# A one-core decoder layer: a third token tile that overlaps the second, state updates taken four sequences at a time, FFN rows fetched at another place, and a new order of the first transfers

## The chip, the cores and the metric

The kernel runs on one core of one Trainium2 chip. The metric is the device time in microseconds (us), the median of several runs; lower is better. Engines are named as the profile names them: PE is TensorE (PEld its weight loads), DVE is VectorE, ACT is ScalarE, POOL is GpSimd, SP is SyncE, which here only starts transfers. All numbers are float32 (`F32`) or the faster matmul form of it (`F32R`).

## The reference, cut to what matters

One step of one decoder layer over 256 prompt tokens (one sequence) and 64 sample tokens (8 sequences of 8 tokens), 320 tokens in all, model width 2048:

```python
u = x @ w_in                                   # 2048 -> 6680: q, k, v, o, two gates, z, xBC, dt
h_m, C, n, m = mlstm_mixer(q, k, v, o, ...)    # 4 heads, 256x256 matrix state per sequence and head
h_s, S, sconv = ssd_mixer(z, xbc, dt, ...)     # 16 heads, 64x128 state per sequence and head
x = layer_norm(ALPHA * x + concat(h_m, h_s) @ w_out)
up = x @ w_up                                  # 2048 -> 11008, then a causal convolution of 3 taps
x = layer_norm(ALPHA * x + (silu(g) * val) @ w_down)

# mLSTM, one sequence (chunk):                 # SSD, one sequence (chunk):
num = (q k' * w_intra) @ v + w_inter * (q @ C) # y = (C B' * decay * dt) @ x + exp(b) * (C @ S)
C_new = decay * C + sum(w_end * k v')          # S_new = exp(b_end) * S + sum(w_end * B x')
```

Every sample sequence brings its own states C and S in and takes new ones out: 8 x 4 matrices of 256x256 and 8 x 16 of 64x128.

## The kernel before, in words

**Main work.** Activations lie transposed, features on partitions and the 320 tokens along the free dimension. Each weight matrix is read in 512 KB pieces (`raw`, four buffers, SP queue, line 61) and split into a rounded part `hi` and a remainder `lo` (ACT line 74, DVE line 75, five buffers each). For every 128x128 weight block three F32R matmuls run: hi times XH, hi times XL, lo times XH (all PE work passes through line 232, or 238 for transposes). There are 9456 such main matmuls: 2496 for `w_in`, 768 for `w_out`, and 6192 for the FFN. A quad is one split, four weight blocks or 12 main matmuls.

**Background work.** Everything else (convolutions, gates, the two mixers, norms) is written as Python generators. After every quad `tasks.pump` lets those run whose due time has come; a due time is the sum of rough matmul costs so far (`tasks.clk`) plus what the generator yielded. So the instruction order of every engine is fixed when the program is written, and PE executes one stream in which short bursts of background matmuls stand between quads. An engine that has to wait holds up all that stands behind it in its own stream.

**Tiles of the 320 tokens.** Tokens 0 to 127 and 128 to 255 are full tiles. The third tile is tokens 256 to 319: 64 rows (`tok(i)` gives 128, 128, 64). It is met in the input transposes (line 412), in the score and decay blocks, in the outputs of both mixers, and in norms.

**The parts the change touches.** `x_transpose` (line 403) turns 16 feature blocks of the input, per block two 128x128 prompt transposes and one of 64 sample rows, in calls of four blocks. `ssd_sample` (line 782): per sequence b, transpose its state, multiply it by its decay on POOL (line 816), add the outer products in `update(b, g)`: four matmuls with 32-row operands in rows 32*(b%4) of the array, to one PSUM bank. `ssd_heads` (line 849) builds per pair of heads the outputs; the sample part is the 64x64 block plus two matmuls with the 0/1 matrix `sel`, which pick 8 of every 32 rows of the state's contribution `yi`. `ml_chunks` (line 1131) does the mLSTM states: two tiles of two sequences per turn, three tiles loaded ahead; four sequences of a turn each get their own two 32-row matmuls. `ml_out` (line 1206) adds, per head, scores times v for the three tiles; the third again fetches `yi` through `sel`. `ffn_consts` (line 1339) fetches convolution rows and weights for the FFN in 512-byte pieces on the POOL queue, waits in due time, and transposes them on PE (line 1347).

**Queues.** Weights, states and big outputs go through SP in order; a transfer there waits for a semaphore of an earlier one or for the engine that frees its buffer. POOL issues small transfers between its arithmetic.

Of the kernel before, what the change touches and what calls it, by code (L numbers as in the profile page):

```python
# [13 lines left out]
NT = 320  # L14
# [7 lines left out]
class Stream:  # L22
# [21 lines left out]
    def load(self, upto=None, own=()):  # L44

        own = list(own)
        while self.nr < len(self.raws) and (own or self.live < self.RB):
# [12 lines left out]
            for c in range(0, m, step):  # L60
                (self.nc.sync if self.nr > 1 else self.nc.scalar).dma_start(t[:, :, c:c + step], src[:, :, c:c + step])
# [109 lines left out]
def _hybrid_step(ctx, tc, I, O):  # L171
# [77 lines left out]
    def tok(i):  # L249
        return 128 if i < 2 else 64  # L250
# [3 lines left out]
    sel = cp.tile([128, 2, 64], F32, name="sel")  # L254
# [58 lines left out]
    def diag3(dg, cols_of):  # L313
        for i in range(3):
            n = tok(i)
            V.tensor_scalar(dg[0:n, i, 0:n], ident[0:n, 0:n], cols_of(i)[0:n], None, ALU.mult)
        return dg

    def colbc(dg):

        ps = bank()
        for i in range(3):
            n = tok(i)
            mm(ps[:, 128 * i:128 * i + n], ones[0:n, :], dg[0:n, i, 0:n], True, True)
        return ps
# [75 lines left out]

    def x_transpose(c, kks=range(4)):
# [4 lines left out]
        for kk in kks:  # L407
# [27 lines left out]
    xs_in = mt("T10", [64, D])  # L435
    for c in range(4):
        x_load(c)
        s = slice(512 * c, 512 * c + 512)
        dma(xs_in[:, s], I["x_sample"].rearrange("b t f -> (b t) f")[:, s])
        if c == 0:  # L440
            src = I["x_prompt"][0, :, 256:512].rearrange("(i p) f -> p i f", p=128)
            dma(box["x", 0][:, :, 256:512], src)
            own = [mt("T4", [128, 1024]) for _ in range(4)]
        st.load(2 * c + 2, (own[0:2], own[2:4], (), ())[c])
# [16 lines left out]

    def load_small():
# [14 lines left out]
        hr = mt("T10", [24, 1536])  # L477
        gdma(hr, I["state_ssm_conv"][0].rearrange("b r c -> (b r) c"))
        gdma(c_tm, I["c_tm"])
        gdma(dsk, I["ssm_D"].broadcast_to([128, 16]))  # L480
        gdma(m01, I["c_m01"])
        gdma(sel, I["c_sel"])
# [5 lines left out]
        for i in range(12):  # L488
            transpose(ps[:, 24 * i:24 * i + 24], hr[:, 128 * i:128 * i + 128])
        A.activation(histx, ps[:, 0:288].rearrange("p (a b) -> p a b", b=24), AF.Copy)  # L490
# [20 lines left out]
    def gate_task(pg):  # L511
        gf, gi = mt("T2", [128, 384]), mt("T2", [4, NT])
        V.memset(gf[:, NT:384], 0.0)
        V.tensor_copy(gf[:, 0:NT], pg[:, 0:NT])
# [5 lines left out]
        for i in range(3):  # L520
            mm(pt[:, 24 * i:24 * i + 24], gf[:, 128 * i:128 * i + 128], fold[:, 0:24], True, True)
        pf = bank()
        mm(pf[0:4, 0:NT], fold[:, 0:4], gf[:, 0:NT], True, True)
# [36 lines left out]
        transpose(pd[0:48, 0:64], dt3[0:64, 2, :])  # L560
# [4 lines left out]
        V.tensor_copy(dtf[32:48], pd[32:48, 0:64])  # L565
# [47 lines left out]
        for i in range(3):  # L613
            transpose(p1[:, 128 * i:128 * i + 128], T1[:, 128 * i:128 * i + 128])
        A.activation(TT1, p1[:, 0:384].rearrange("p (a b) -> p a b", b=128), AF.Copy)
        p2 = bank()
# [59 lines left out]
    def ssd_cb():  # L676
# [4 lines left out]
        for g in range(2):  # L681
# [3 lines left out]
            mm(ps[0:64, 384:448], B[:, g, 256:NT], C[:, g, 256:NT], True, True)  # L685
            t = mt("T2", [128, 448])
            G.memset(t[64:128, 384:448], 0.0)
            V.tensor_tensor(t[:, 0:384], ps[:, 0:384], m01[:, 0:384], ALU.mult)
            V.tensor_tensor(t[0:64, 384:448], ps[0:64, 384:448], m01[0:64, 384:448], ALU.mult)
# [76 lines left out]
    def ssd_xdt():  # L766
# [3 lines left out]
        for i in range(3):  # L770
            n = tok(i)
            for hh in range(2):
                ps = bank()
                for j in range(4):
                    transpose(ps[0:n, 128 * j:128 * j + 128], XS[:, 4 * hh + j, 128 * i:128 * i + n])
                V.tensor_tensor(by(xdt[0:n, i, 512 * hh:512 * hh + 512], 64), by(ps[0:n, :], 64),
                                bcl(dt3[0:n, i, 32 + 8 * hh:40 + 8 * hh], 64), ALU.mult)
                yield 500
        box["xdt"] = xdt
        flags.add("xdt")  # L780

    def ssd_sample():
# [19 lines left out]
        yield from wait("bc")  # L802
        load(0)
        load(1)
        yield from wait("x4")
        yi = {}
        for b in range(8):
            t = tiles[b]
            sts[b] = mt("T4", [128, 8, 128])
            for g in range(2):  # L810
# [6 lines left out]
                yield 1000  # L817
            if b:
                update(b - 1, 0)
                yield 500  # L820
                update(b - 1, 1)
                yield 1000
            if b > 1:
                dma(s_dst[b - 2].rearrange("(j q) n -> q j n", q=128), tiles.pop(b - 2))
            if b < 6:
                load(b + 2)
            if b % 4 == 3:
                x = b // 4
                for g in range(2):
                    ps = bank()  # L830
                    for c in range(4):
                        w = sts[4 * x + c][:, 4 * g:4 * g + 4, :].rearrange("p j n -> p (j n)")
                        mm(ps[32 * c:32 * c + 32, :], box["cz"][:, g, 4 * x + c, :], w, True, True)
                    y = mt("T2", [128, 512])
                    V.tensor_tensor(by(y, 64), by(ps, 64), bcl(eb[:, x, 8 * g:8 * g + 8], 64), ALU.mult)
                    yi[g, x] = y
                    yield 0
                sts.clear()
        update(7, 0)
        yield 0  # L840
        update(7, 1)
        box["yi"] = yi
        flags.add("yi")
        yield
        for b in (6, 7):
            dma(s_dst[b].rearrange("(j q) n -> q j n", q=128), tiles.pop(b))

    def ssd_heads():
# [41 lines left out]
        for j in range(8):  # L890
# [47 lines left out]
    def ssd_norm():  # L938
        var = sm([128, 3, 2])
        G.memset(var, 1.0)  # L940
        for g in range(2):
# [10 lines left out]
            for i in range(3):  # L952
                mm(ps[0:tok(i), 2 * i:2 * i + 2], sq[:, 128 * i:128 * i + tok(i)], ones[:, 0:2], True, True)
            pv = ps[:, 0:6].rearrange("p (a b) -> p a b", b=2)
# [771 lines left out]
```

## Time and profile before

| | |
|---|---|
| runs, median (lowest to highest) | 1579.27 us (1578.6 to 1581.3) |
| the profiled execution's own time | 1580.12 us |
| its span, first to last instruction | 1578.3 us |
| PE / PEld / DVE / ACT / POOL busy, share of the span | 98% / 95% / 62% / 49% / 18% |
| granted TensorE clock, mean | 0.992 |
| moved by transfers | 253.97 MB, 161 GB/s over the span |

A row of the timeline gives start and length in us, engine, line, what was computed from what, partitions x elements and a count; in brackets the idle time ahead of it and what ended it. Because matmuls are pipelined, the time one costs PE is the distance from its start to the next start, not its own length. A transpose or an F32R matmul is one record, a full float32 matmul is two. A timeline row can gather forms that differ under the first one's name (a run of 64-row and 128-row transposes has one row). Rows of stretches give, per engine, busy time and records, then the granted clock, the busy share of the transfer engines, and GB/s.

### The profile page before, as it was taken

Reading aid. Unit: us, or ns where it says so; the run is one execution under the profiler, and the core shown is the slowest. Engines: PE = TensorE matmul, PEld = TensorE weight load, DVE = VectorE, ACT = ScalarE, POOL = GpSimd, SP = SyncE. Lnnn points to the kernel's source line nnn. Section 1 sums busy time; section 2 is a strip of 40 time slices with the busy share of each in tenths; the row PEclk is TensorE's granted clock in tenths of the full one; section 3 lists DMA queues with packets and bytes.
Section 4 is the critical chain, followed back from the end, with each engine's and each line's share of the span. In section 5 each row is a group of like instructions: output and inputs, shape, how many; then the busy total and the mean of one; then the engine's idle time right before and its main releaser. Section 6 shows DMA issues by size and latency. Waiting matters only on the chain.

```text
span 1578.3 us, 27987 instructions
## 1 busy us (share of the span) xinstructions
PE 1553.8 (98%) x10547; PEld 1502.5 (95%) x10547; DVE 976.6 (62%) x1957; ACT 773.1 (49%) x1532; POOL 290.3 (18%) x601
## 2 busy tenths in 40 slices
PE   9999999999999997999999999999999999999997
PEld 7999999998889997999999999999999999999996
DVE  5775445656677585687777545565644465556765
ACT  3665433435445453476666435555533455555332
POOL 4213220024311073133321000000000000001301
PEclk9999999999999998999999999999999999999998
DMA  9456665577665566445554455455444545455642
GB/s 260 147 161 160 187 187 172 143 193 208 195 221 183 169 183 138 134 147 149 149 151 135 157 158 146 148 156 152 136 152 144 167 145 151 143 154 168 170 140 79
DMA packets 267080, 253.97 MB, mean 161 GB/s; under 512 B 18804, under 2 KB 261263, under 8 KB 266816
## 3 DMA queue, kind: packets, MB, share of 16 engines
q1 hardware_dynamic: 260432, 246.76, 53.2%
q0 software_dynamic: 4928, 4.37, 1.3%
q8 instruction: 82, 1.34, 0.3%
q10 hardware_dynamic: 1584, 1.05, 0.3%
q14 instruction: 54, 0.44, 0.1%
HBM read 231.63 MB, written 20.43 MB: 160 GB/s over the span
## 4 chain that ended last, share of the span: by engine, by line
PE 86%; issue 7%; DMA 2%; POOL 1%; DVE 1%; ACT 1%; POOLq 0%; SPq 0%; DVEq 0%; ACTq 0%
PE bk L232 84%; PE bk L238 2%; DMA rows<-ffn_conv_w 1%; POOL T L425 1%; DMA raw<-w_out 1%; DVE lo L75 1%; DMA T<-ln_g 0%; DMA gbias<-ssm_dt_bias 0%; DMA xT<-T 0%; POOL big L1654 0%; ACT hi L74 0%; DVE big L1393 0%; DVE big L1389 0%; ACT L657 0%; ACT T L644 0%
## 5 line engine op out<-in xcount | busy, mean ns | idle before, releaser
L75 DVE TENSOR_TENSOR lo<-raw,hi 128x512 fp32r<-128x512 f32 (+2 forms) x800 | 556.4, 706 | 391.7 <-ACT hi L74 389.3
L74 ACT ACTIVATE hi<-raw 128x512 fp32r<-128x512 f32 (+2 forms) x800 | 486.3, 616 | 455.9 <-PE bk L232 427.3
L232 PE MATMUL bk<-big,hi 128*128 128x320 f32 (+1 forms) x2752 | 609.3, 310 | 0.0
L232 PEld LDWEIGHTS bk<-big,hi 128*128 128x128 f32 x2752 | 462.2, 188 | 0.1
L232 PE MATMUL bk<-big,lo 128*128 128x320 f32 (+1 forms) x1376 | 426.5, 310 | 0.0
L232 PE MATMUL bk<-XH,hi 128*128 128x320 f32 x832 | 270.2, 325 | 0.1
L232 PEld LDWEIGHTS bk<-big,lo 128*128 128x128 f32 x1376 | 259.3, 188 | 0.0
L232 PE MATMUL bk<-XH,lo 128*128 128x320 f32 x832 | 258.2, 310 | 0.1
L232 PE MATMUL bk<-XL,hi 128*128 128x320 f32 x832 | 258.0, 310 | 0.0
L232 PE MATMUL bk<-HH,hi 128*128 128x320 f32 x688 | 214.2, 311 | 0.0
L232 PE MATMUL bk<-HH,lo 128*128 128x320 f32 x688 | 212.6, 309 | 0.0
L232 PE MATMUL bk<-HL,hi 128*128 128x320 f32 x688 | 212.5, 309 | 0.0
L232 PEld LDWEIGHTS bk<-XH,hi 128*128 128x128 f32 x832 | 157.2, 189 | 14.7 <-issue 5.5
L232 PEld LDWEIGHTS bk<-XL,hi 128*128 128x128 f32 x832 | 157.4, 189 | 0.4
L232 PEld LDWEIGHTS bk<-XH,lo 128*128 128x128 f32 x832 | 157.2, 189 | 0.6 <-DVE lo L75 0.6
L1492 DVE SCALAR_TENSOR_TENSOR c<-c,fcol,c 128x336 f32<-128x336 f32 x172 | 98.0, 570 | 58.6 <-ACT c L1490 55.6
L232 PEld LDWEIGHTS bk<-HL,hi 128*128 128x128 f32 x688 | 129.2, 188 | 0.0
L232 PEld LDWEIGHTS bk<-HH,hi 128*128 128x128 f32 x688 | 129.2, 188 | 0.0
L232 PEld LDWEIGHTS bk<-HH,lo 128*128 128x128 f32 x688 | 129.1, 188 | 0.0
L193 POOL TENSOR_SCALAR fst<-c 128x18 f32<-128x18 f32 x86 | 22.2, 265 | 567.4 <-ACT c L1485 567.4
L232 PE MATMUL bk<-MH,hi 128*128 128x320 f32 x256 | 80.9, 316 | 0.0
L232 PE MATMUL bk<-MH,lo 128*128 128x320 f32 x256 | 80.1, 313 | 0.7 <-DVE lo L75 0.7
(338 smaller groups left out, 1505.8 us busy)
## 6 DMA issues: line engine op xcount, KB each, us to landing
raw<-ffn_w_up SPq DMA_DIRECT2D x172, 512.0 KB, 3.8
raw<-w_in SPq DMA_DIRECT2D x100, 512.0 KB, 4.1
raw<-ffn_w_down SPq DMA_DIRECT2D x71, 512.0 KB, 3.6
raw<-w_out SPq DMA_DIRECT2D x32, 512.0 KB, 3.9
T<-state_mlstm_C SPq DMA_DIRECT2D x32, 256.0 KB, 5.8
s_C<-T SPq DMA_DIRECT2D x32, 256.0 KB, 4.9
T<-state_ssm SPq DMA_DIRECT2D x8, 512.0 KB, 6.5
s_ssm<-T SPq DMA_DIRECT2D x8, 512.0 KB, 5.3
```

What stands on the lines that cost most here:

```text
L74: nc.scalar.activation(h, src, AF.Copy)
L75: nc.vector.tensor_tensor(l, src, h.bitcast(F32), ALU.subtract)
L193: G.tensor_scalar(out, in_, 1.0, 0.0, ALU.mult, ALU.add)
L232: nc.tensor.matmul(out, lhsT=lhsT, rhs=rhs, start=start, stop=stop)
L238: nc.tensor.transpose(out, in_, ident[b:b + p, b:b + p])
L425: G.tensor_tensor(t, f32(XH(k, 2)), f32(XL(k, 2)), ALU.add)
L1492: V.scalar_tensor_tensor(c[:, 0:336], xp[:, j:j + 336], fcol[:, j, i:i + 1], c[:, 0:336], ALU.mult, ALU.add)
```

## The change

- **Third token tile.** It becomes tokens 192 to 319, 128 rows of which the last 64 (partitions 64 to 127) are the sample tokens. `tok` goes, `TS` gives the three slices. The first 64 rows are duplicates of tokens 192 to 255; in the two places where a sum runs over them they carry something else (next point).
- **State contributions.** In both mixers `yi` is no longer added through `sel`. Four small POOL transfers per tile (`gather`) copy 8 of every 32 rows into the free partitions 0 to 63 of the third tile of `xdt` or `VT`, and the matching 64x64 block of the weights is the identity. One matmul then does both.
- **State updates of four sequences.** `ssd_sample` decays four states, then issues 16 update matmuls per half with the sequence as the inner loop, into four banks; `ml_chunks` issues the eight of a turn likewise, half outside, sequence inside. Four chunk tiles are loaded ahead, and stored and reloaded two at a time.
- **Input.** Sample rows are loaded as 128 partitions (feature halves above each other), so that a transpose serves blocks k and k+8. The first weight pieces move from the ACT queue to SP, the identity and the first sample rows from SP to ACT; nine warm-up matmuls instead of seven.
- **FFN rows.** `ffn_consts` starts its transfers after 12000 instead of 25000 of due time and waits 40000 instead of 20000 before it transposes.

The diff, cut to its core (norms, scores, the final transposes and LN2 use `TS` in the same way):

```diff
-                (self.nc.sync if self.nr > 1 else self.nc.scalar).dma_start(t[:, :, c:c + step], src[:, :, c:c + step])
+                self.nc.sync.dma_start(t[:, :, c:c + step], src[:, :, c:c + step])
-    def tok(i):
-        return 128 if i < 2 else 64
+    TS = (slice(0, 128), slice(128, 256), slice(192, NT))
...
-    for _ in range(7):
+    for _ in range(9):
         mm(warm[:, 0:128], ones, ones, True, True)
...
-            dma(ident, I["c_ident"])
+            nc.scalar.dma_start(ident, I["c_ident"])
...
-            transpose(ps[:, 256:NT], xs_in[:, 128 * k:128 * k + 128])
-            A.activation(XH(k), ps[:, 0:NT], AF.Copy)
-            V.tensor_tensor(XL(k), ps[:, 0:NT], f32(XH(k)), ALU.subtract)
+            parts = [(k, 0, 256)]
+            if k < 8:
+                transpose(ps[:, 256:384], xs_in[:, 128 * k:128 * k + 128])
+                parts = [(k, 0, NT), (k + 8, NT, 384)]
...
+    x_load(0)
+    xs_load(nc.scalar, 0, 256)
+    own = [mt("T4", [128, 1024]) for _ in range(4)]
+    st.load(1, own[0:1])
+    dma(box["x", 0][:, :, 256:512], I["x_prompt"][0, :, 256:512].rearrange("(i p) f -> p i f", p=128))
+    xs_load(nc.sync, 256, 512)
+    st.load(2, own[1:2])
...
+    def gather(out, y):
+        for c in range(4):
+            gdma(out[8 * c:8 * c + 8], y[32 * c:32 * c + 8])
...
-        def update(b, g):
-            v = tiles[b][:, 4 * g:4 * g + 4, :]
-            ps = bank()
-            r = slice(32 * (b % 4), 32 * (b % 4) + 32)
-            for j in range(4):
-                mm(ps[:, 128 * j:128 * j + 128], box["X4"][b // 4][r, 4 * g + j, :], box["B4"][r, b // 4, g, :],
-                   True, True)
-            V.tensor_tensor(v, v, ps.rearrange("p (j n) -> p j n", n=128), ALU.add)
+        def update(x, g):
+            pss = [bank() for _ in range(4)]
+            for j in range(4):
+                for c in range(4):
+                    r = slice(32 * c, 32 * c + 32)
+                    mm(pss[c][:, 128 * j:128 * j + 128], box["X4"][x][r, 4 * g + j, :], box["B4"][r, x, g, :],
+                       True, True)
+            tasks.clk -= 12 * 108
+            for c in range(4):
+                v = tiles[4 * x + c][:, 4 * g:4 * g + 4, :]
+                V.tensor_tensor(v, v, pss[c].rearrange("p (j n) -> p j n", n=128), ALU.add)
+                if g:
+                    dma(s_dst[4 * x + c].rearrange("(j q) n -> q j n", q=128), tiles.pop(4 * x + c))
...
+                gather(box["xdt"][32 * x:32 * x + 32, 2, 512 * g:512 * g + 512], y)
...
-            for x in range(2):
-                mm(ps[:, 256:NT], box["yi"][g, x][:, 128 * (j % 4):128 * (j % 4) + 128], sel[:, x, :], x == 0, False)
             for e, (p, f) in enumerate(pe):
-                mm(ps[p, 256:NT], xdt[0:64, 2, f], mw[e][0:64, 384:448], False, True)
+                mm(ps[p, 256:NT], xdt[:, 2, f], mw[e][:, 384:448], True, True)
             for i in range(2):
-                mm(po, xw[:, i, :], btok[:, i, g, :], i == 0, i == 1)
+                for e, (p, f) in enumerate(pe):
+                    mm(po[p, :], xw[:, i, p], btok[:, i, g, :], i == 0, i == 1)
...
-        for n in range(3):
+        for n in range(4):
             load(n)
...
-                box["yi", h, x] = yi
+                gather(box["VT"][32 * x:32 * x + 32, 2, h, 0:257], yi[:, 0:257])
                 yield 500
+                pss = [bank() for _ in range(4)]
+                for e in range(2):
+                    for b in range(4):
+                        r = slice(32 * b, 32 * b + 32)
+                        mm(pss[b][:, 256 * e:256 * e + 256], kv[r, 0, x, 128 * e:128 * e + 128], kv[r, 1, x, :], True, True)
...
-        mm(ps[0:64, 0:257], P[0:64, 384:448], VT[0:64, 2, h, 0:257], True, False)
-        for x in range(2):
-            mm(ps[0:64, 0:257], sel[:, x, :], box.pop(("yi", h, x))[:, 0:257], False, x == 1)
-        A.activation(num[0:64, 2, 0:257], ps[0:64, 0:257], AF.Copy)
+        mm(ps[:, 0:258], P[:, 384:512], VT[:, 2, h, :], True, True)
+        A.activation(num[:, 2, :], ps[:, 0:258], AF.Copy)
...
     def ffn_consts():
-        yield 25000
+        yield 12000
...
-        yield 20000
+        yield 40000
```

In the program's order the change shows at two places on which the prediction rests. The first is PE, one pair of SSD heads (`ssd_heads`). Names before the arrow are the bank written, after it the moving and then the stationary operand's tile; the numbers are the program's buffer numbers. Before:

```order
L232 MATMUL bk_2964<-T_240_2829,T_156_1738 64x256
L232 MATMUL bk_2964<-T_241_2834,T_156_1738 64x256
L232 MATMUL bk_2964<-T_240_2829,T_156_1738 64x128
L232 MATMUL bk_2964<-T_241_2834,T_156_1738 64x128
L232 MATMUL bk_2964<-sel,T_202_2288 128x64
L232 MATMUL bk_2964<-sel,T_233_2733 128x64
L232 MATMUL bk_2964<-T_240_2829,T_156_1738 64x64
L232 MATMUL bk_2964<-T_241_2834,T_156_1738 64x64
L232 MATMUL bk_2964<-T_149_1720,T_242_2839 128x128 x2
L232 MATMUL bk_2862<-XH_368,hi_2881 128x320
```

And now, for such a pair:

```order
L232 MATMUL bk_2951<-T_243_2799,T_156_1730 64x256
L232 MATMUL bk_2951<-T_244_2804,T_156_1730 64x256
L232 MATMUL bk_2951<-T_243_2799,T_156_1730 64x128
L232 MATMUL bk_2951<-T_244_2804,T_156_1730 64x128
L232 MATMUL bk_2951<-T_243_2799,T_156_1730 64x64
L232 MATMUL bk_2951<-T_244_2804,T_156_1730 64x64
L232 MATMUL bk_2951<-T_149_1712,T_245_2809 64x128 x4
L232 MATMUL bk_2934<-XH_165,hi_2864 128x320
```

The two `sel` matmuls are gone, the 64x64 pair stays (its operands now have 128 rows, which the row does not say), and two full-width matmuls have become four that write 64 columns each.

The second place is POOL at the start of the `w_out` stage, around the FFN rows. `c` are the running sums of the first layer norm (d and its square), `big` is d. Before:

```order
L193 TENSOR_SCALAR c_6271<-big_6268 128x320
L1400 TENSOR_TENSOR c_6271<-c_6271,big_6268 128x320
L1403 TENSOR_TENSOR c_6272<-c_6272,c_6470 128x320
L1400 TENSOR_TENSOR c_6271<-c_6271,big_6268 128x320
L1403 TENSOR_TENSOR c_6272<-c_6272,c_6512 128x320
```

Eight more such rows stand there, and then the transfers `rows_6636<-state_ffn_conv`, `rows_6645<-ffn_conv_w` and `rows_6645<-ffn_conv_b`. And now:

```order
L193 TENSOR_SCALAR c_6323<-big_6320 128x320
L1365 DMA rows_6502<-state_ffn_conv 86x2x128 x8
L1367 DMA rows_6511<-ffn_conv_w 86x3x128
L1368 DMA rows_6511<-ffn_conv_b 86x128
L1422 TENSOR_TENSOR c_6323<-c_6323,big_6320 128x320
L1425 TENSOR_TENSOR c_6324<-c_6324,c_6534 128x320
```

The ten transfers have moved ahead of twelve additions. On PE the first transposes of these rows stood after 3048 main matmuls and stand after 3096.

More of the change, by code (lines that the diff above doesn't have):

```diff
@@ L321, in colbc @@
         ps = bank()
-        for i in range(3):
-            n = tok(i)
-            mm(ps[:, 128 * i:128 * i + n], ones[0:n, :], dg[0:n, i, 0:n], True, True)
+        for i in range(2):
+            mm(ps[:, TS[i]], ones, dg[:, i, :], True, True)
+        mm(ps[:, 256:NT], ones, dg[:, 2, 64:128], True, True)
         return ps
@@ L433, in keep_x, with xs_load @@
         yield from gate_task(pg)
[L435 to L444, printed above, removed]
+    xs_in = mt("T10", [128, 1024])
+    xs_src = I["x_sample"].rearrange("b t f -> (b t) f")
+    def xs_load(eng, a, b):
+        for e in range(2):
+            eng.dma_start(xs_in[64 * e:64 * e + 64, a:b], xs_src[:, 1024 * e + a:1024 * e + b])
+    x_load(0)
[5 more added lines that the diff above has]
+    st.load(2, own[1:2])
+    x_load(1)
+    st.load(3, own[2:3])
+    xs_load(nc.sync, 512, 1024)
+    st.load(4, own[3:4])
+    x_load(2)
+    st.load(6)
+    x_load(3)
+    st.load(8)
     gw = mt("T2", [128, 16, 32])
@@ L460, in _hybrid_step, with swapped @@
     n0f = sm([128, 64], name="n0f")
+    def swapped(out, in_):
+        for e in range(2):
+            gdma(out[64 * e:64 * e + 64], in_[64 - 64 * e:128 - 64 * e])
     def load_small():
@@ L487, in load_small @@
         ps = bank()
-        for i in range(12):
-            transpose(ps[:, 24 * i:24 * i + 24], hr[:, 128 * i:128 * i + 128])
-        A.activation(histx, ps[:, 0:288].rearrange("p (a b) -> p a b", b=24), AF.Copy)
+        for a in range(3):
+            transpose(ps[:, 96 * a:96 * a + 96], hr[:, 128 * a:128 * a + 128])
+        A.activation(histx.rearrange("p (q a) b -> p a q b", a=3), ps[:, 0:288].rearrange("p (a q b) -> p a q b", a=3, b=24),
+                     AF.Copy)
         d2 = dsk.rearrange("p (j e) -> p j e", e=2)
@@ L770, in ssd_xdt @@
         for i in range(3):
[L771 removed]
+            p = slice(64 * (i == 2), 128)
             for hh in range(2):
@@ L791, in load, with decay @@
             tiles[b] = t
-        def update(b, g):
-            v = tiles[b][:, 4 * g:4 * g + 4, :]
-            ps = bank()
-            r = slice(32 * (b % 4), 32 * (b % 4) + 32)
-            for j in range(4):
-                mm(ps[:, 128 * j:128 * j + 128], box["X4"][b // 4][r, 4 * g + j, :], box["B4"][r, b // 4, g, :],
-                   True, True)
-            V.tensor_tensor(v, v, ps.rearrange("p (j n) -> p j n", n=128), ALU.add)
[L802 to L807, printed above, removed]
+        def decay(b):
             t = tiles[b]
@@ new lines, in ssd_sample @@
+        yield from wait("bc")
+        load(0)
+        load(1)
+        yield from wait("x4", "xdt")
+        for x in range(2):
+            for c in range(4):
+                b = 4 * x + c
+                if c < 2 and b + 2 < 8:
+                    load(b + 2)
+                decay(b)
+                yield 2500
+            for g in range(2):
+                ps = bank()
+                for c in range(4):
+                    w = sts[4 * x + c][:, 4 * g:4 * g + 4, :].rearrange("p j n -> p (j n)")
+                    mm(ps[32 * c:32 * c + 32, :], box["cz"][:, g, 4 * x + c, :], w, True, True)
+                tasks.clk -= 3 * 865
+                y = mt("T2", [128, 512])
+                V.tensor_tensor(by(y, 64), by(ps, 64), bcl(eb[:, x, 8 * g:8 * g + 8], 64), ALU.mult)
+                gather(box["xdt"][32 * x:32 * x + 32, 2, 512 * g:512 * g + 512], y)
+                yield 0
+            sts.clear()
+            if x == 0:
+                load(4)
+                load(5)
+            for g in range(2):
+                update(x, g)
+                yield 2500
@@ L1251, in ml_out @@
             ps = bank()
-            for i in range(3):
-                transpose(ps[:, 128 * i:128 * i + tok(i)], num[0:tok(i), i, 128 * e:128 * e + 128])
+            for i in (2, 0, 1):
+                transpose(ps[:, TS[i]], num[:, i, 128 * e:128 * e + 128])
             A.activation(Q[:, 2 * h + e, :], ps[:, 0:NT], AF.Copy, scale=col(C_NM + 2 * h + e))
@@ L1532, in down_task @@
         if j == 2 and m == 15:
-            for i in range(3):
-                t = slice(128 * i, 128 * i + tok(i))
+            for t in (slice(0, 128), slice(128, NT)):
                 V.tensor_tensor(a[:, t], a[:, t], ps[:, t], ALU.add)
```

182 lines of the change are left out of this document (71 added, 111 removed).

## The prediction

> **What bounds the kernel now.** I read the page's busy shares first, then the chain that ended last, then a stretch of the FFN that holds nothing but main work.
>
> ```profile
> PE 1553.8 (98%) x10547; PEld 1502.5 (95%) x10547; DVE 976.6 (62%) x1957; ACT 773.1 (49%) x1532; POOL 290.3 (18%) x601
> PE 86%; issue 7%; DMA 2%; POOL 1%; DVE 1%; ACT 1%; POOLq 0%; SPq 0%; DVEq 0%; ACTq 0%
> 800.00:1000.00 200.00, 200.00 (x1361) 200.00 (x1361) 119.24 (x228) 103.77 (x210) 21.91 (x59) 1.00 0.49 148
> ```
>
> PE sets the end. The third row (length; busy of PE, PEld, DVE, ACT, POOL; clock; transfers) gives 200/1361 = 0.147 us from one main matmul to the next. Both kernels hold 9456 of them, 1390 us. What can go is the background bursts between quads and the few places where PE waits. I price a burst by what it adds: start of the second main behind it, less start of the last main ahead, less 2 x 0.147.
>
> **The bursts that get shorter.** A burst of twelve input transposes, four of them of 64 rows, and a later burst of twelve of 128 rows:
>
> ```profile
> 19.02 2.30 PE L238 MATMUL bk<-ident,T 128*128 128x128 f32 x12
> 21.25 0.41 PE L232 MATMUL bk<-XH,hi 128*128 128x320 f32 x1
> 21.50 0.30 PE L232 MATMUL bk<-XL,hi 128*128 128x320 f32 x1
> ...
> 140.84 1.47 PE L238 MATMUL bk<-ident,T 128*128 128x128 f32 x12
> 142.07 0.39 PE L232 MATMUL bk<-XH,hi 128*128 128x320 f32 x1
> ```
>
> The last main ahead started 0.147 before the first row, so that burst adds 21.50 - 19.02 - 0.147 = 2.33; the second takes 1.23 to the next main, with the slower step behind it about 1.31, 0.11 per transpose. So a 64-row transpose costs about 0.36, and three bursts become 12, 8 and 8 whole ones: 1.31 + 0.87 + 0.87 for 7.0. **Saves 3.9.**
>
> SSD update of one sequence, four 32-row matmuls in one row group:
>
> ```profile
> 165.26 0.31 PE L232 MATMUL bk<-XH,lo 128*128 128x320 f32 x1
> 165.50 0.66 PE L232 MATMUL bk<-T,T 32*128 32x128 f32 x4
> 166.09 0.42 PE L232 MATMUL bk<-XH,hi 128*128 128x320 f32 x1
> 166.34 0.31 PE L232 MATMUL bk<-XL,hi 128*128 128x320 f32 x1
> ```
>
> It adds 0.79; the 16 updates (two in one burst) add 12.2. Four bursts of 16 take their place. If the four row groups ran wholly beside each other, a burst would still cost 0.79 (saves 9.0); if nothing overlapped, some 2.1 (saves 3.8); with the matmuls together and their weight loads one behind another, 1.4. The nearest row is the mLSTM chunk below, where two row groups do overlap. I take 1.2. **Saves 7.5.**
>
> One pair of SSD heads:
>
> ```profile
> 254.27 0.31 PE L232 MATMUL bk<-XH,lo 128*128 128x320 f32 x1
> ...
> 255.31 0.66 PE L232 MATMUL bk<-sel,T 128*128 128x64 f32 x4
> 255.90 0.97 PE L232 MATMUL bk<-T,T 64*64 64x64 f32 x8
> 256.62 0.39 PE L232 MATMUL bk<-XH,hi 128*128 128x320 f32 x1
> 256.86 0.30 PE L232 MATMUL bk<-XL,hi 128*128 128x320 f32 x1
> ```
>
> It adds 2.30. The `sel` matmuls (255.90 - 255.31 = 0.59) go; the 64x64 pair, now of 128 rows, is about 0.1 cheaper (an estimate, from the 64-row transposes above). I count the four half-width state matmuls as the two whole ones before. About 1.60 remains, eight times: **saves 5.5** (4.9 to 6.3).
>
> Third tile of the mLSTM outputs, one head:
>
> ```profile
> 387.06 0.31 PE L232 MATMUL bk<-XH,lo 128*128 128x320 f32 x1
> ...
> 387.87 1.08 PE L232 MATMUL bk<-T,sel 128*64 128x257 f32 x4
> 388.88 0.42 PE L232 MATMUL bk<-XH,hi 128*128 128x320 f32 x1
> 389.13 0.31 PE L232 MATMUL bk<-XL,hi 128*128 128x320 f32 x1
> ```
>
> It adds 1.78. One whole matmul of 258 columns takes its place, two passes: 0.44. Four heads: **saves 5.4.**
>
> mLSTM state update, two sequences:
>
> ```profile
> 378.09 0.31 PE L232 MATMUL bk<-XH,lo 128*128 128x320 f32 x1
> 378.33 0.50 PE L232 MATMUL bk<-T 32*128 32x256 f32 x4
> 378.76 0.42 PE L232 MATMUL bk<-XH,hi 128*128 128x320 f32 x1
> 379.01 0.31 PE L232 MATMUL bk<-XL,hi 128*128 128x320 f32 x1
> ```
>
> It adds 0.63, 16 times 10.1. Four matmuls of 256 columns in 0.43 is two passes of about 0.22 each: the two sequences of a pair run together. With four sequences, 8 bursts of eight cost 0.63 (all four together) to 1.25 (pairs only). I take 0.75: **saves 4.1** (0 to 5.0).
>
> *Skill.* The Trainium skill, "TensorE: Matmul & The Clock Gate", Part 3 (packing small matmuls), says that matmuls in different row groups run at once, weight loads too, and gives 3.07 times for four tiles of 512 columns. The chunk row agrees for two groups. By it both updates would sit at their lower ends, some 2.5 us below my sum.
>
> Smaller ones: a burst of six final transposes (two of 64 rows) adds 1.19 and becomes six of 128 rows, 0.65, four times, 2.2:
>
> ```profile
> 492.25 1.15 PE L238 MATMUL bk<-ident,T 128*128 128x128 f32 x6
> ```
>
> In the same way, estimated from the 64-row and 128-row prices above: the decay columns 1.4, convolution history 0.7, SSD score blocks 0.5, scores 0.6, merged state products 0.7, norm sums 0.5. **Saves 6.6.** PE work together: 3.9 + 7.5 + 5.5 + 5.4 + 4.1 + 6.6 = 33.0; with all lower ends 24.7, all upper ends 35.9.
>
> **The FFN rows.** `c<-big` is the first sum of the norm; POOL starts the rows at 576.06, and PE waits for them from 593.52:
>
> ```profile
> 551.81 0.46 POOL L193 TENSOR_SCALAR c<-big 128x320 f32<-128x320 f32 x1 [36.45 <-DMA raw<-w_out]
> ...
> 576.06 12.80 POOL L1343 DMA_DIRECT2D rows<-state_ffn_conv  x8
> ...
> 590.69 0.56 POOL L1346 DMA_DIRECT2D rows<-ffn_conv_b  x1
> ...
> 593.52 0.31 PE L232 MATMUL bk<-MH,lo 128*128 128x320 f32 x1
> 602.09 0.83 PE L238 MATMUL bk<-ident,rows 86*128 86x86 f32 x4 [8.27 <-DMA rows<-ffn_conv_w]
> 603.07 0.47 PE L232 MATMUL bk<-ML,hi 128*128 128x320 f32 x1
> ...
> 602.00:607.20 5.20, 5.11 (x21) 5.11 (x22) 2.04 (x5) 0.63 (x1) 0.00 (x0) 0.50 0.17 56
> ...
> rows<-ffn_conv_w POOLq DMA_DIRECT2D x1, 129.0 KB, 13.2
> ```
>
> The stall and its cold transposes add 603.07 - 593.52 - 0.29 = 9.25 against 0.34 for a like burst at full clock: 8.9. Then 21 records in 5.2 us at clock 0.50 instead of 3.1 are some 2.2 late. Together 11.1. In the new order POOL reaches the block (590.69 + 0.56 - 576.06 = 15.2 us of issuing) right behind that first sum, 552.3 to 567.5 on the old clock; 13.2 us of landing is 581, and the transposes stand 48 mains (7 us) later than before, at 600. Slack 20 us: **saves 11.1.**
>
> What the block now stands in front of are the norm's POOL additions. Eight of them (0.84 each, 6.8 us) have their inputs by the time POOL is free and then run back to back. What such a row does to DVE stands at the old place:
>
> ```profile
> 592.21 4.85 DVE L75 TENSOR_TENSOR lo<-raw,hi 128x512 fp32r<-128x512 f32 x2 [2.22 <-ACT hi L74]
> ...
> 593.66 0.84 POOL L1403 TENSOR_TENSOR c<-c,c 128x320 f32<-128x320 f32 x1
> ...
> 598.11 0.63 ACT L74 ACTIVATE hi<-raw 128x512 fp32r<-128x512 f32 x1 [5.42 <-DMA raw<-w_out]
> ...
> L75 DVE TENSOR_TENSOR lo<-raw,hi 128x512 fp32r<-128x512 f32 (+2 forms) x800 | 556.4, 706 | 391.7 <-ACT hi L74 389.3
> ```
>
> Two splits took 4.85 us instead of 1.4 while POOL added without a gap, and `hi` waited 5.42 us for a weight piece while the rows' small packets were under way: two delays that the old stall covered. At the new place nothing covers them but PE's lead, five `lo` buffers, some four quads of 12 x 0.147, 7 us. DVE held for 6.8 us plus late pieces is at the edge of it. I book a **new stall of 4** (1 to 9).
>
> *Skill.* The Trainium skill, "SBUF — State Buffer", section "SBUF: two separate sides", has a DVE operation on two SBUF inputs and a GpSimd operation exclude each other for the whole instruction. The 4.85 us agrees. By it alone DVE is out for 6.8 us of a lead of 7: 0 to 2 us of stall.
>
> **Start, and other waits.** The first transposes wait for the identity and the sample rows:
>
> ```profile
> 7.42 1.27 PE L238 MATMUL bk<-ident,T 64*128 64x64 f32 x4 [1.29 <-DMA T<-x_sample]
> ```
>
> Both moved to another queue; the first weights moved behind the input on SP. I take 1 saved (1 lost to 3 saved). Four state tiles in hand at once, 512 KB loads behind 512 KB stores on SP, and four banks taken in one burst can each make PE wait once: 2 lost (0 to 6).
>
> **The sum.** 33.0 + 11.1 - 4 + 1 - 2 = 39.1. The profiled execution took 1580.1, the median is 0.85 below: 1541.0 and **1540 us**. With PE's work at 28 to 35 and the new stalls at 4 to 10, its own range is 1533 to 1548.
>
> **Rivals.**
> - *Row groups overlap no further than in pairs.* SSD bursts 1.6 to 2.1, chunk bursts 1.25: 7.7 less, **1548**. For it: the trace shows pairs and no four. Against: in the chunk row two groups run beside each other at no visible price, and nothing in it hints at an end there.
> - *The FFN rows stall PE at the new place*, by held additions and late pieces, long enough for a half clock behind it as at 602: 7 more, **1547**; if the rows come late again after all, 1551. For it: the 4.85 and 5.42 us. Against: 20 us of slack for the rows themselves.
> - *Nothing new waits* and four groups run as one: 35.9 + 11.1 + 1 = 48, **1531**.
> - *The gather becomes PE's wait, slower.* The third tile's matmul of each mLSTM head now needs an ACT copy, four POOL issues and their landing. From the matmul that makes `yi` to the one that reads it lie 72 to 108 mains in the new order, 13 to 16 us with the bursts between. The nearest row, beside the issue of 0.56 at 590.69:
>
> ```profile
> s_n<-T POOLq DMA_DIRECT2D x1, 32.0 KB, 1.8
> ```
>
>   0.5 + 4 x 0.56 + 1.8 is 4.5 us, and with the slowest landing of POOL's queue, 13.2 as above, 16. To cancel the gain, PE would have to wait 10 us at each of four heads, a chain of 23 to 26 us; at 25 us with the half clock behind each wait it is 4 x 14.6 = 58 more, **1599**. Against it: the queue is hardly used at that time.
>
> **How the numbers follow.** The sum 58%, pairs only 12%, stall at the new place 15%, nothing waits 12%, gather 3%. The range 1529 to 1556 takes in the first four with their bounds and leaves out the gather and the corners. A measurement here tells about 0.2%, 3.2 us, from no change. The first four cases are all over 20 us faster; 0.95 faster, 0.02 same, 0.03 slower.
>
> **What would show it.** In the timeline after: SSD update bursts that add 0.8 to 1.4; pairs of heads 1.6; third tiles 0.44; chunk bursts of eight under 0.9; no idle time at the first `ident,rows` transposes. Clock 1.00 from about 17 us to the last norm, or else a stall between 515 and 565 with `lo` or `raw` named, the place I trust least. PE waits on a transfer between two `T` buffers would show the gather. The FFN matmuls behind it should take what they took. I am wrong if PE's idle time in the first 560 us is over 15 us, or if bursts of 16 cost over 2.

## The result, and the profile after

| | before | changed kernel |
|---|---|---|
| median (lowest to highest) | 1579.24 us (1578.6 to 1581.3) | 1551.72 us (1549.1 to 1554.9) |
| the profiled execution's own time / its span | 1580.12 / 1578.3 | 1549.13 / 1547.4 |

The ratio is 0.982 (95% interval 0.980 to 0.985): 27.5 us faster. The forecast was 1540, 39 us faster, with a range to 1556. The direction and most of the mechanism came as forecast; a third of the gain is missing. The page of the changed kernel:

```profile
PE 1517.5 (98%) x10518; PEld 1485.9 (96%) x10518; DVE 982.5 (63%) x1959; ACT 773.4 (50%) x1540; POOL 318.1 (21%) x661
PE 94%; DMA 2%; DVE 1%; SPq 1%; POOL 0%; issue 0%; ACT 0%; POOLq 0%; ACTq 0%; DVEq 0%
```

PE has 36 us less work and the chain that ended last still runs through it, but PE is not busier than before: 98% of a shorter span. What it waits for is another list now. Its waits in the changed kernel (sum, times, longest):

```profile
PE bk L232 <- DVE lo L75: 4.7, 3, 3.2
PE bk L238 <- DVE fsm L1651: 4.5, 1, 4.5
PE bk L232 <- ACT hi L74: 3.2, 2, 2.2
PE bk L232 <- DMA T<-w_in: 3.0, 1, 3.0
PE bk L238 <- DMA T<-state_ssm: 2.6, 1, 2.6
```

The 8.3 us for the FFN rows are gone from it; the second row was there before (4.5, the last norm); the other four are new or grown. What follows in the list is 1.8 or less.

Both kernels run the same 9456 main matmuls in the same order, so the start of the n-th one (counted from 0) in each trace tells where time was won and lost. Worked out from the two traces' single records; the text below calls this table the ladder and main matmuls mains:

| main matmul | before, us | changed, us | ahead by | what lies in between |
|---|---|---|---|---|
| 84 | 30.62 | 26.65 | 4.0 | start, two bursts of input transposes |
| 108 | 35.10 | 35.58 | -0.5 | first gate burst |
| 2496 | 509.27 | 484.04 | 25.2 | both mixers, the rest of `w_in` |
| 2788 | 555.53 | 528.04 | 27.5 | start of `w_out` |
| 3028 | 590.73 | 569.82 | 20.9 | first layer norm |
| 3076 | 609.24 | 576.86 | 32.4 | FFN rows in the kernel before |
| 9455 | 1559.38 | 1527.12 | 32.3 | FFN |
| end of span | 1578.3 | 1547.4 | 31.0 | last norm, outputs |

**PE's bursts.** The rows that answer to those of the prediction: input transposes, one SSD update burst, one pair of heads, one third tile, one chunk burst.

```profile
17.51 1.48 PE L238 MATMUL bk<-ident,T 128*128 128x128 f32 x12
18.74 0.39 PE L232 MATMUL bk<-XH,hi 128*128 128x320 f32 x1
18.97 0.30 PE L232 MATMUL bk<-XL,hi 128*128 128x320 f32 x1
...
175.96 0.31 PE L232 MATMUL bk<-XH,lo 128*128 128x320 f32 x1
176.20 0.67 PE L232 MATMUL bk<-T,T 32*128 32x128 f32 x16
176.79 0.41 PE L232 MATMUL bk<-XH,hi 128*128 128x320 f32 x1
177.05 0.31 PE L232 MATMUL bk<-XL,hi 128*128 128x320 f32 x1
...
234.45 0.31 PE L232 MATMUL bk<-XH,lo 128*128 128x320 f32 x1
234.69 1.42 PE L232 MATMUL bk<-T,T 128*64 128x256 f32 x20
236.04 0.41 PE L232 MATMUL bk<-XH,hi 128*128 128x320 f32 x1
236.29 0.31 PE L232 MATMUL bk<-XL,hi 128*128 128x320 f32 x1
...
359.44 0.31 PE L232 MATMUL bk<-XH,lo 128*128 128x320 f32 x1
359.59 0.60 PE L232 MATMUL bk<-T,T 128*128 128x258 f32 x2
359.83 0.50 PE L232 MATMUL bk<-XH,hi 128*128 128x320 f32 x1
360.17 0.31 PE L232 MATMUL bk<-XL,hi 128*128 128x320 f32 x1
...
348.26 0.31 PE L232 MATMUL bk<-XH,lo 128*128 128x320 f32 x1
348.50 0.51 PE L232 MATMUL bk<-T 32*128 32x256 f32 x8
348.93 0.41 PE L232 MATMUL bk<-XH,hi 128*128 128x320 f32 x1
349.18 0.31 PE L232 MATMUL bk<-XL,hi 128*128 128x320 f32 x1
```

By the same price (second main behind, less last main ahead, less 0.29; ahead of the transposes the last main started 0.15 earlier) they add 1.32, 0.80, 1.55, 0.44 and 0.63 us. Sixteen SSD update matmuls now cost what four cost before. Over all bursts, with the stalls named below taken out, it is 146.3 us before and 109.4 now: 36.9 less.

**The new waits.** In the timeline: the first gate burst in the kernel before (first row), and in the changed kernel that burst, the SSD states and a weight piece behind their stores, and the first norm.

```profile
32.57 0.75 PE L232 MATMUL bk<-T,T 128*32 128x320 f32 x8
...
31.60 1.30 PE L232 MATMUL bk<-T,T 128*32 128x320 f32 x8 [2.95 <-DMA T<-w_in]
...
181.93 5.25 SPq L848 DMA_DIRECT2D s_ssm<-T  x4
189.58 0.80 SPq L821 DMA_DIRECT2D T<-state_ssm  x1
196.29 1.09 PE L238 MATMUL bk<-ident,T 128*128 128x128 f32 x8 [2.61 <-DMA T<-state_ssm]
230.54 0.41 PE L232 MATMUL bk<-XH,hi 128*128 128x320 f32 x1 [2.25 <-ACT hi L74]
...
542.20 3.55 DVE L1415 SCALAR_TENSOR_TENSOR big<-big,cols,big 128x320 fp32r<-128x320 f32 x1
545.67 2.89 DVE L75 TENSOR_TENSOR lo<-raw,hi 128x512 fp32r<-128x512 f32 x1
547.16 0.85 POOL L1422 TENSOR_TENSOR c<-c,big 128x320 f32<-128x320 f32 x1
548.61 0.41 PE L232 MATMUL bk<-MH,lo 128*128 128x320 f32 x1 [1.34 <-DVE lo L75]
550.00 1.01 DVE L1415 SCALAR_TENSOR_TENSOR big<-big,cols,big 128x320 fp32r<-128x320 f32 x2
555.57 0.42 PE L232 MATMUL bk<-MH,lo 128*128 128x320 f32 x1 [3.18 <-DVE lo L75]
```

The gate weights landed at 32.0 us in the kernel before and at 31.5 now. And the stretches behind the first and the last of these waits (length, busy times of PE, PEld, DVE, ACT and POOL, granted clock, transfers): the clock is down to 0.89 and 0.72.

```profile
33.00:41.00 8.00, 7.50 (x47) 7.26 (x48) 2.45 (x5) 2.31 (x6) 0.00 (x0) 0.89 0.67 210
555.50:559.00 3.50, 3.43 (x17) 3.43 (x18) 3.49 (x7) 0.63 (x1) 0.00 (x0) 0.72 0.57 170
```

DVE's `DL` operation (line 1415) takes 0.5 us each at 550.00, with two in 1.01. At 542.20 one took 3.55, and the split behind it 2.89, while POOL ran nine additions without a gap from 540.07 to 548.01; DVE's second long one ended at 548.56, half a microsecond behind POOL's last. PE then waited twice for `lo`, and lost some more at a lower clock behind the second wait: 6.6 us in the ladder. The FFN rows' first transposes no longer wait, and add 0.34:

```profile
579.80 0.46 PE L238 MATMUL bk<-ident,rows 86*128 86x86 f32 x4
```

**The balance of the profiled executions.** Won: 36.9 in bursts and 10.8 at the FFN rows (8.9 of stall and 1.9 at the lower clock behind it; the ladder's 11.5 holds 0.7 of transposes that the changed kernel makes behind main 3076). Lost: gate weights 4.5 (3.8 in the burst, 0.7 in mains at the lower clock behind it), the input transposes behind them 0.7 (PE waits 0.5 there for DVE's `XL`, also in the last run below, where the gate weights come in time), the state load 2.8, the weight piece near 230 2.9, the first norm 6.6, the end 1.3 (from the last main matmul to the end 19.0 before and 20.2 now). The kernel before with only the rows moved takes 20.1 for that end, so the new tiles do not make it; its cause is open. That leaves 28.9 of the 31.0. Of the other 2.1, the earlier start is 0.4, the mains up to 84 are 0.3, and 1.3 lie between mains 2496 and 2788, where the kernel before waits 0.7 for `lo`. The median lies 2.6 above this profiled execution; the first run below shows what varies.

### The profile page after: what moved, and what is told of

Same layout as the page of the kernel before. It is cut to its first block, busy times and chain, and to the rows that moved or that the text cites. A ratio compares the mean times of both kernels' runs of the same rounds, so it can differ in the third digit from the quotient of the medians.

```text
span 1547.4 us, 28114 instructions
## 1 busy us (share of the span) xinstructions
PE 1517.5 (98%) x10518; PEld 1485.9 (96%) x10518; DVE 982.5 (63%) x1959; ACT 773.4 (50%) x1540; POOL 318.1 (21%) x661
## 4 chain that ended last, share of the span: by engine, by line
PE 94%; DMA 2%; DVE 1%; SPq 1%; POOL 0%; issue 0%; ACT 0%; POOLq 0%; ACTq 0%; DVEq 0%
PE bk L232 92%; PE bk L238 2%; DMA T<-w_in 1%; SPq L61 0%; DMA T<-state_ssm 0%; DVE lo L75 0%; DMA T<-x_prompt 0%; DMA raw<-w_in 0%; DVE big L1415 0%; DMA T<-x_sample 0%; POOL big L1670 0%; SPq L466 0%; SPq L394 0%; DVE big L1411 0%; DVE big L1428 0%
```

## The experiments

All medians are from four executions (eight for the kernel before with the rows moved), each set beside runs of the kernel before, whose medians stayed within 1578.9 and 1579.2.

### The changed kernel again

No edit.

> The changed kernel once more, beside the others of this set. Its four executions so far spread over 1549.1 to 1554.9 us, the kernel before over 1578.6 to 1581.3. Theory: the four stalls of its first profile come back at the same places (3.0 us at 31.6 for the gate weights, 2.6 at 196.3 for a state load, 2.4 near 229 for a weight piece, 4.8 and a cold stretch near 548 to 555), the transfer ones by one or two us more or less; 1549 to 1555. Rival: the stalls are chance of one execution, and another profile shows other places.

Measured: 1551.54 us (1548.6 to 1555.0), its profiled execution 1555.0. The stalls of the first profile stand at the same places, and one more. At the gate weights:

```profile
PE bk L232 <- DMA T<-w_in: 5.0, 1, 5.0
```

5.0 instead of 3.0; from main matmul 84 to 120 this execution loses 3.2 us on the first one, and 1.4 more from 960 to 1300, at the state load and the weight piece. The new place is the first step of the norm: the first piece of the residual input `rx` landed 7.1 us after its issue instead of 4.6, and from main 2692 to 2788 this execution loses 3.7, of which the stall of the norm behind it gives 1.9 back. So much of the spread of the changed kernel (6 us, against 3 before) is in landings of transfers that PE now waits for.

### FFN rows at the old place

```diff
 def ffn_consts():
-    yield 12000
+    yield 25000
 ...
-    yield 40000
+    yield 20000
```

> The changed kernel with the FFN rows fetched and transposed at the old place. Theory (held additions): the stall near 548 to 555 (6.6 us with its cold stretch) is caused by the rows' block on POOL and goes, the old stall at the rows' transposes comes back (8.9 + 2.2 = 11.1): 4.5 us slower than the changed kernel, about 1556. Rival (the shorter PE stream left the norm behind by itself): the stall near 550 stays, 11 us slower, 1563.

Measured: 1556.39 us, 4.85 slower than the changed kernel in the same set. PE's first wait is the old one:

```profile
PE bk L238 <- DMA rows<-ffn_conv_w: 8.2, 1, 8.2
```

From main 2692 to 3028 this kernel takes 51.8 us, the changed one 56.4, the one before 51.2. The stall of the first norm comes and goes with the place of the rows, as the theory has it.

### The same move in the kernel before

```diff
-    yield 25000
+    yield 12000
 ...
-    yield 20000
+    yield 40000
```

> The kernel before with nothing changed but the two waits of the FFN rows (12000 and 40000 of due time). Theory: PE's 8.9 + 2.2 us at the rows' transposes go, and POOL's held additions make the new stall here as they do in the changed kernel (6.6 us): 4.5 us faster, about 1574.5, with PE waiting for lo near 578 to 586. Rival (the held additions hurt only behind the changed kernel's shorter stream): 10 to 11 us faster, about 1568.5.

Measured: 1574.38 us, ratio 0.9968 (0.9958 to 0.9978), 4.5 faster. PE's first wait:

```profile
PE bk L232 <- DVE lo L75: 4.8, 3, 3.1
```

The move is worth 4.5, not 11: it pays for the stall it removes with the one it makes, in the old kernel as in the new. It owes nothing to the shorter stream: from main 2788 to 3028 this kernel takes 41.6 us, the changed one 41.8, the one before 35.2.

### The norm's additions on DVE

```diff
-        e = V if m == 15 else G
+        e = V
```

> The changed kernel with the 28 additions of the first layer norm that POOL made now made by DVE (0.49 us each, in DVE's idle time). The rows' transfers stay where they are. Theory (POOL's back-to-back additions hold DVE): no DVE instruction of several us near 542 to 548, no wait of PE for lo there, 5 to 6.6 us faster than the changed kernel, about 1546. Rival (weight pieces come late because the rows' small packets are under way): PE still waits near 545 to 555, now for hi and a weight piece, and the time stays within 1.5 us.

Measured: 1547.72 us (1544.5 to 1551.5), 3.8 faster than the changed kernel, with executions that overlap. The trace is plainer than the median: mains 2692 to 3028 take 50.8 us instead of 56.4, and DVE's instructions there are short, though it does POOL's work as well:

```profile
547.00 0.69 DVE L75 TENSOR_TENSOR lo<-raw,hi 128x512 fp32r<-128x512 f32 x1
547.61 0.55 DVE L1415 SCALAR_TENSOR_TENSOR big<-big,cols,big 128x320 fp32r<-128x320 f32 x1
548.07 0.48 DVE L1422 TENSOR_TENSOR c<-c,big 128x320 f32<-128x320 f32 x1
```

An addition is 0.48 on DVE. The rows' transfers and their packets are where they were, so it is the additions on POOL, and not late weight pieces, that made this stall. The Trainium skill, "SBUF — State Buffer", section "SBUF: two separate sides", says that a DVE operation on two SBUF inputs and a GpSimd operation that reads SBUF lock each other out for a whole instruction; the 3.55 us operation under POOL's additions and the 0.55 without them agree that the two exclude each other. POOL's additions take 0.8 to 1.1 each here, so DVE was passed over for more than one of them.

### The rows at the start of the stage

```diff
-    yield 12000
+    yield 0
 ...
-    yield 40000
+    yield 52000
```

> The changed kernel with the FFN rows fetched 12000 of due time earlier, at the start of the w_out stage, and transposed where the change has it. POOL does nothing then, so the 15 us of issuing stand ahead of the first sum of the norm and hold no addition. Theory (held additions): the stall near 548 to 555 is gone, 6 to 6.6 us faster than the changed kernel, about 1545. Rival (late weight pieces): the stall moves with the rows' transfers to about 500 to 520 and keeps 3 us or more, 1548 to 1552.

Measured: 1550.75 us, 0.8 faster, within the spread. The `lo` wait is gone, as the theory says, but a new one stands at the norm's first step, which is the kind the rival named, with another transfer:

```profile
524.59 1.68 DVE L1398 SCALAR_TENSOR_TENSOR big<-rx,bk 128x320 f32<-128x320 f32 x4 [12.94 <-DMA rx<-xT]
525.18 1.41 PE L232 MATMUL bk<-big,ones 128*128 128x320 f32 x2 [5.97 <-issue]
```

`rx`, the residual input, was issued at 512.4 and used at 524.6; in the changed kernel it was issued at 513.3 and used at 518.0. Its first piece landed 12.1 us after its issue, with the rows' pieces landing up to 521.5; in the other thirteen traces that takes 4.6 to 7.5, and where it takes 6.9 or more PE waits 0.8 to 1.4 us at this step. Against the first profile this run wins 6.3 us from main 2788 to 3028 and loses 8.3 from 2692 to 2788. So both delays of the prediction show: held additions where the block stands ahead of additions, and a late load where it stands ahead of one that something waits for at once. That the rows' pieces are what holds `rx` up rests on this one run.

### Row groups: another order

```diff
-            for j in range(4):
-                for c in range(4):
+            for c in range(4):
+                for j in range(4):
```

and likewise in `ml_chunks`.

> The changed kernel with its update matmuls in another order: all of a sequence (one row group) behind each other, then the next sequence; the same matmuls, banks and sums. Theory (the four row groups overlap only because neighbours in the stream differ): a burst of 16 SSD updates costs 1.9 to 3.1 us instead of 0.79, a chunk burst of eight 1.0 to 1.3 instead of 0.63; 4 x 1.1 to 2.3 plus 8 x 0.4 to 0.7, so 7 to 14 us slower than the changed kernel, 1559 to 1565. Rival (the queue of PE finds the free row groups by itself, whatever the order): both bursts unchanged, 1551.

Measured: 1551.35 us, no difference. A burst:

```profile
176.55 0.31 PE L232 MATMUL bk<-XH,lo 128*128 128x320 f32 x1
176.79 0.70 PE L232 MATMUL bk<-T,T 32*128 32x128 f32 x16
177.42 0.41 PE L232 MATMUL bk<-XH,hi 128*128 128x320 f32 x1
177.67 0.31 PE L232 MATMUL bk<-XL,hi 128*128 128x320 f32 x1
```

It adds 0.83 instead of 0.80. The theory as I put it falls: neighbours in the stream need not differ.

### Row groups: one group for all

Every sequence of a group of four gets the update of its first one, so this kernel leaves out the updates of the other three; the number and the shapes of the matmuls stay.

```diff
-                    r = slice(32 * c, 32 * c + 32)
+                    r = slice(0, 32)
```

> The changed kernel with all 16 matmuls of each SSD update burst in the same 32 rows of the array: every sequence of a group of four gets the update of its first one, so states of the other three are not the reference's; instructions, banks and burst places stay. Theory (the overlap of row groups makes the saving, and it needs different rows, not a certain order): a burst costs 2.0 to 2.4 us instead of 0.79, four bursts 5 to 6.5 us, about 1557. Rival (the saving is that four short bursts became one, with one entry and one exit): a burst stays under 1.2, 1551 to 1553.

Measured: 1555.31 us, 3.8 slower than the changed kernel, and the burst:

```profile
177.60 0.31 PE L232 MATMUL bk<-XH,lo 128*128 128x320 f32 x1
177.84 2.00 PE L232 MATMUL bk<-T,T 32*128 32x128 f32 x16
179.77 0.42 PE L232 MATMUL bk<-XH,hi 128*128 128x320 f32 x1
180.02 0.31 PE L232 MATMUL bk<-XL,hi 128*128 128x320 f32 x1
```

2.13 us. Four such bursts are 5.3 us more than the changed kernel's; the wait for the state load behind them is 1.2 instead of 2.6, which gives part of it back. Four separate bursts of the kernel before are 4 x 0.79 = 3.2, one burst in one group 2.1, one burst in four groups 0.8: of 2.4 us saved, 1.0 comes from standing in one burst instead of four, 1.3 from the groups running beside each other. The order within the burst gives nothing.

### The state transfers in another order

```diff
+        def store(b):
+            dma(s_dst[b].rearrange("(j q) n -> q j n", q=128), tiles.pop(b))
...
-                if g:
-                    dma(s_dst[4 * x + c].rearrange("(j q) n -> q j n", q=128), tiles.pop(4 * x + c))
+                if g and not x:
+                    store(c)
...
-                if c < 2 and b + 2 < 8:
+                if b < 2:
                     load(b + 2)
+                if b == 4:
+                    load(7)
...
                 load(5)
+                load(6)
...
         flags.add("yi")
+        for b in range(4, 8):
+            store(b)
+            yield 2500
```

> The changed kernel with the SSD state transfers in another order on SP: the load of sequence 6 ahead of the four stores of the first group instead of behind them, that of sequence 7 one step earlier, and the last four stores spread over four steps instead of issued together. Theory (four 512 KB stores in a row hold SP and the transfers behind them): the wait of 2.6 us at 196 for a state load and that of 2 to 2.4 us near 227 for a weight piece go, 4 to 5 us faster than the changed kernel, about 1547. Rival (transfers as a whole are the limit there, 180 to 230 GB/s): the waits move by a few us and stay, within 1.5 us of it.

Measured: 1544.22 us (1542.2 to 1545.7), 7.3 faster than the changed kernel and more than expected. The wait for a state load is gone from PE's list, and from main 960 to 1300 it takes 59.3 us instead of 65.1. A load behind four stores of 512 KB, and four stores issued together, where the kernel before issued them one by one, were the cause; the two halves of the edit were not run apart. The medians differ by more than the trace's 5.8; part of that is spread.

### Three edits together, and the gate weights

The gate burst delayed, with the two edits that had worked:

```diff
-            yield 1000 if c else 8000
+            yield 1000 if c else 14000
```

> The changed kernel with three edits together: the norm's additions on DVE, the state transfers in the other order, and the first gate burst 6000 of due time later, behind the landing of the gate weights. Theory (all the new waits are separate and none hides another): 1551.5 less 6 (norm), 4 to 5 (states) and 3.5 to 4.5 (gate), 1536 to 1539, and PE's only waits of over 1 us are at the start and in the last norm. Rival (a wait removed lets PE run into the next transfer): 1541 to 1546, with waits for raw or for other gate weights.

Measured: 1540.39 us. The wait for the gate weights is gone and 4.6 us are won by main 360, but PE then waits in the mLSTM stage for score blocks:

```profile
PE bk L232 <- DVE T L1086: 3.9, 2, 2.5
```

The same without the delay:

> The changed kernel with the norm's additions on DVE and the state transfers in the other order, and the gate burst where the change has it. Theory (delaying the gate burst only moved its 4 us to the mLSTM stage, where PE waited 3.9 us for a DVE result): 1544.2 less the 4 to 6 of the norm, 1538 to 1540, the same as with the delayed gate burst. Rival (the delay is a real gain and the mLSTM wait has another cause): 1543 to 1545.

Measured: 1537.87 us (1535.5 to 1542.1), 2.5 below the one with it (1539.3 to 1541.1), with executions that overlap. The delay only moved the wait: by main 960 the delayed kernel is 5.1 us ahead of this one, by 2496 it is 2.8 behind. The gate weights themselves, issued at the start on ACT's queue:

```diff
     xs_load(nc.scalar, 0, 256)
...
+    nc.scalar.dma_start(gw[:, :, 0:8], w[:, :, 4096:4104])
+    nc.scalar.dma_start(gw[:, :, 8:24], w[:, :, 6664:6680])
...
     st.load(8)
...
-    dma(gw[:, :, 0:8], w[:, :, 4096:4104])
-    dma(gw[:, :, 8:24], w[:, :, 6664:6680])
```

> As the one before, and the gate weights fetched at the start on ACT's queue, behind the identity and the first sample rows, instead of on SP behind the weight pieces. Theory (PE waits at 31.6 for the landing alone): no wait there, no cold stretch behind it, 3.5 to 5 us faster than the one before, 1534 to 1536. Rival (at the start the transfers as a whole are the limit: their thousands of small pieces delay the input or the first weights): the wait moves ahead, first main later than 8.4 or waits for raw up to 25 us, 1537 to 1541.

Measured: 1537.53 us, no gain. The wait moved to the sample rows, as the rival says:

```profile
PE bk L238 <- DMA T<-x_sample: 4.9, 2, 3.2
```

And on SP, ahead of weight pieces they used to follow:

```diff
     x_load(2)
...
+    dma(gw[:, :, 0:8], w[:, :, 4096:4104])
+    dma(gw[:, :, 8:24], w[:, :, 6664:6680])
     st.load(6)
     x_load(3)
     st.load(8)
...
-    dma(gw[:, :, 0:8], w[:, :, 4096:4104])
-    dma(gw[:, :, 8:24], w[:, :, 6664:6680])
```

> As the one before the last, with the gate weights on SP but two weight pieces and one input piece earlier (behind the third input piece). Theory: their landing moves from 31.5 to about 24 us and the wait goes; the two weight pieces behind them come some 3 us later, which costs 0 to 3: 1535 to 1539. Rival as for the ACT queue: PE waits for raw instead, 1538 to 1542.

Measured: **1533.62 us** (1532.7 to 1535.3), ratio to the kernel before 0.9715 (0.970 to 0.973), 18 us faster than the changed kernel. The gate weights now land at 23.8, and of PE's waits only the last norm's is over 1.2 us:

```profile
PE bk L238 <- DVE fsm L1660: 4.5, 1, 4.5
```

## Why the prediction was right or wrong

**PE's bursts: right, and a little low.** Forecast 33.0 (24.7 to 35.9), measured 36.9, above the upper end. (The terms' own ends add up to 24.6 and 36.2, not 24.7 and 35.9.) Input transposes 3.9 as forecast. SSD updates 9.0 (12.2 less four of 0.80) instead of 7.5: I priced a burst at 1.2, between "groups overlap" and "weight loads one behind another", and the first end is what holds; the Trainium skill's packing rule ("TensorE: Matmul & The Clock Gate", Part 3), which I set aside as some 2.5 us, was right. Chunks likewise, 5.0 instead of 4.1. Heads 6.0 instead of 5.5, third tile 5.4 as forecast. The small ones come to about 7.6 instead of 6.6. The reason that I gave for the SSD number before the last runs held in one half only: they show that the matmuls must lie in different groups, but not that neighbours in the stream must.

**FFN rows: right.** 10.8 for 11.1 of old stall.

**The held additions: right mechanism, price within its bounds.** Forecast 4 (1 to 9), measured 6.6, and shown by three runs: it follows the rows in the old kernel, goes with them in the new, and goes when DVE makes the additions. The term was sized by DVE alone being out for 6.8 us of a lead of 7. It left out that DVE has its own work queued behind those 6.8 us, and that POOL has a second batch at 550.6, so PE waited a second time, with a drop of the clock behind it.

**Start and other waits: the step that failed.** "I take 1 saved" and "2 lost (0 to 6)": one saved and two lost, against 5.2 lost at the gate weights and the transposes behind them, 5.7 at state transfers, and 1.3 at the end. One of the prediction's own signs of being wrong came with it: in the first 560 us PE was idle for 16.9 us (4.6 in the kernel before), more than the 15 it named. The state transfers were named, at the right place, and priced at one short wait each, inside the range; in the run they cost 5.7, and their other order won 5.8 there. The gate weights were not named at all. In the kernel before they landed 0.6 us ahead of their burst (and 0.9 us late in the kernel before with the rows moved), and now they land only 0.5 us earlier, so what was won ahead of it, by shorter transposes and the earlier start, was lost to it: the ladder's 4.0 at main 84 is -0.5 at main 108. I counted the saving of the transposes at full in a stretch where PE was level with its transfers; that is where the expected gain of the start went.

**The sum and the rivals.** 33.0 + 11.1 - 4 + 1 - 2 became, by the profiled executions, 36.9 + 10.8 less 18.8, with 2.1 at the start and ahead of the first norm; by the median 2.6 more are gone, much of which, by the second profile, is in landings. That the total stayed this near the forecast is in part luck: 3.9 us of bursts priced too low stand against the missed waits. "Row groups overlap no further than in pairs" is refuted by the 0.80; "nothing new waits" by the list of waits. "The FFN rows stall PE at the new place" is the rival that came nearest, by mechanism and by its clock. The gather never showed: the third tile at 359.59 has no wait, and its four transfers had landed by 353.8. The result, 1551.7, lies within the range and outside the likeliest case's own, 1533 to 1548 (1536 to 1549 when its terms, 28 to 35 of PE's work and 4 to 10 of new stalls, are added up again).

## What to carry to other kernels

When a change shortens the bounding engine's stream, list what lands just in time around it: each landing behind which no slack was left eats what is won ahead of it, and the gain shows only once that transfer is moved too. A block of transfers that an engine issues costs what stands behind it on that engine and in the queues: look for additions that pile up, for loads with one quick user, and for stores issued four together. And packing pays in different rows of the array and in fewer bursts, not in the order in which the matmuls are written.

## What the runs showed of the hardware that was not expected

- Matmuls in different row groups run beside each other even when four of one group stand together in the stream (0.83 us for 16, against 2.13 in one group). In the single records of the other-order run the first four of the 16 start within 0.04 us of each other, and the four that start last are the four that signal a finished bank. In the stream these are the 4th, 8th, 12th and 16th, so the starts do not follow the stream's order; the records do not name the row group.
- While POOL ran nine additions back to back, DVE got through two instructions in the 6.4 us from 542.20 on: one of 0.5 us took 3.55 and one of 0.69 took 2.89. With all the additions on DVE, 0.48 each, PE's mains 2692 to 3028 take 50.8 us instead of 56.4.
- With the FFN rows' many small pieces under way, the first piece of the residual input `rx` landed 12.1 us after its issue, against 4.6 to 7.5 in the other thirteen traces. One run shows it.
